# S5's early prompt parts ahead of the sample's projections, its reorder copies on ScalarE, and eight memsets on VectorE

## Chip, core and metric

The kernel runs on one core of one Trainium2 chip. The metric is the device time of one launch in microseconds (us); several runs are taken, and the median counts. Tiles live in the core's on-chip memory, matmuls run on TensorE (PE), and VectorE (DVE), ScalarE (ACT) and GpSimd (POOL) do the elementwise work. Every engine works through a list of its own, in order. SyncE (SP) issues most DMAs, POOL some.

## What is computed

One layer of a hybrid trunk, for a prompt of 4096 frames and for a sample of 32 frames of a running stream. A normalised input h goes through one projection. Half of it feeds a gated delta rule with 4 heads (a 4-tap convolution on q, k and v, then a recurrence in blocks), the other half a diagonal state-space group (S5), each with a gate path; both are joined, mapped by an output projection and added to x.

```
h = rms_norm(x)
q, k, v, beta, gates, z, z5, u = split(h @ W_in)
q, k, v = silu(short_conv(q, k, v))          # 4 taps
S_t = exp(g_t) (I - beta_t k_t k_t^T) S_{t-1} + beta_t k_t v_t^T ;  o_t = S_t^T q_t
x_t = Lbar x_{t-1} + Bbar u_t ;  y_t = Re(C x_t) + D u_t       # S5
y5 = gelu(y) * sigmoid(y @ W_glu + b) * silu(z5)
out = x + concat(o * silu(z), y5) @ W_out
```

## The kernel before, in words

The kernel has three phases. Phase A makes h, stores it, and computes what S5 needs (uts, gy_d and gys_d in DRAM). Phase B, where the change lies, runs the delta rule and the output gate of S5. Phase C is the output projection.

In phase B a small driver (`Drive`) takes pieces of work from generators and emits them: one called `dense`, and four (`chunks`) that share 33 chunks of the recurrence, 128 frames each, with the sample's chunk as number 32. A generator's `yield` says when it may go on, and the driver decides by a model of matmul time which one is next. The order in which it emits is then reordered by the framework's scheduler, so that the final lists of the engines are not the order of the source.

`dense` is a list of block projections and of S5 units in between. `qkv(b)` (L1370) projects 256 frames of block b onto k, q and v, 4 heads each, from two tiles of h that `load_h` (L1358) reads transposed on SP (L1366). `qkv_s` (L1414) does the same for the sample's 32 frames, with gyt and zr as working room. `s5out(k, j)` (L1460) is one S5 unit of 128 frames: gyt is loaded (L1455), zr holds z5 (L1458), gyt is split into two f16 parts gh (L224, L225), four transposes on PE (L53), twelve matmuls with the weights wg (L49), some elementwise work (L1484 to L1495) and a store (L1497). There are 32 such units of the prompt, and one of the sample, whose gyt is first reordered by two copies (L1475, L1476). `useq` is the order of the units; a unit loads the unit that comes two later, because there are two rooms.

z, the gate of the delta rule (L534, `zproj`), is filler for PE with a low priority and a set of transposed h loads of its own (L561). `chunk` (L1512) builds a chunk: bl and dm are loaded on SP (`load_be`, L1505; `load_dm`, L1510), their product br and its mask run on POOL (L1605, L1609), sk and rq_k normalise k and q (L135 to L139 on POOL), the casts kn (L1586) and vb (L1595) run on ACT, then follow products and an inverse by doubling steps on PE and DVE, for which POOL makes a (L1715). Of the inverse tiles p1bd, p1f, ap32 and ap64 there are two each, cleared once by `masks` (L1300, memsets at L1356), before the loops.

Constants: SP = 2 (the sample's chunk comes after two blocks), EARLY = 4, LATE = 4.

Of the kernel before, what the change touches and what calls it, by code (L numbers as in the profile page):

```python
# [26 lines left out]
SP = 2  # L27
# [5 lines left out]
EARLY = 4  # L33
# [47 lines left out]
class Trunk:  # L81
# [1077 lines left out]
    def phase_b(self):  # L1159
        nc, io, cst = self.nc, self.io, self.cst  # L1160
        NB = self.T // 256
        b2 = ExitStack()
        self.ck = self.pool(b2, "b_ck")
        wm = self.pool(b2, "b_m")
        self.pg = [self.pool(b2, f"b_pg{i}", 1, psum=True) for i in range(NI)]
        self.po = self.pool(b2, "b_po", 1, psum=True)
        self.pf = self.pool(b2, "b_pf", 1, psum=True)
        self.S = {}
        for key in ("p", "s"):
            self.S[key] = wm.tile([128, H, 128], F32, name=f"S_{key}")  # L1170
        nc.gpsimd.memset(self.S["p"], 0.0)
        nc.sync.dma_start(self.S["s"], io["state_dn"])
        self.bounds(wm)
        q0 = self.blk[0, "q"]
        nc.gpsimd.tensor_scalar(q0, q0, self.sq["p"], None, op0=ALU.mult)
        self.masks(wm)
        self.ncv = {key: cst.tile([128, 3, 12], F32, name=f"ncv_{key}") for key in ("p", "s")}
        self.nu = 0
        self.front, self.chain, self.busy, self.slots = set(), -1, False, list(range(NI))
        items = [(i, i % 2, i // 2, "p") for i in range(2 * NB)]  # L1180
        items.insert(2 * SP, (self.NC, 0, -1, "s"))
        self.dms, self.sdone = {}, False
        self.order = [i[0] for i in items]
        self.load_be(self.order[0])
        for i in items[:NP]:
            self.load_dm(i[0])
        items = [items[p::NP] for p in range(NP)]
        self.at = [0] * NP
        self.early = list(range(NE))

        def dense():
            units = [(k, j) for k in range(NB // 4) for j in range(8)]
            self.useq = units[:2] + [(-1, 0)] + units[2:]
            late = units[len(units) - LATE:]
            units = units[:len(units) - LATE]
            for b in list(range(1, SP)) + [-1] + list(range(SP, NB)):
                if b == 2:
                    for u in units[:EARLY]:
                        yield from self.s5out(*u)
                    units = units[EARLY:]  # L1200
                if b > 1:
                    yield lambda: {2 * b - 4, 2 * b - 3} <= self.front
                yield from self.qkv(b) if b >= 0 else self.qkv_s()
                for u in units[:2] if b >= 0 else [(-1, 0)]:
                    yield from self.s5out(*u)
                if b >= 0:
                    units = units[2:]
            self.b1.close()
            self.c_weights()
            for u in units + late:  # L1210
                yield from self.s5out(*u)
            self.fn = self.wz.tile([128, 2, 4, 512], F16, name="wg").rearrange("p x c n -> p (x c n)").bitcast(F32)[:, :1024]
            nc.sync.dma_start(self.fn, io["final_norm_w"].partition_broadcast(128))
            xe = [self.hp.tile([128, 8, 272], F16, name=f"h{i % 2}").rearrange("p c n -> p (c n)").bitcast(F32)[:, :1024] for i in range(4)]
            for j, b in enumerate(self.early):
                yield from self.out(b, lambda i: xe[(2 * j + i) % 4],
                                    lambda: self.rm["gh"][:, 0].bitcast(BF16),
                                    lambda: self.pb.tile([128, 512], F32, name="pp"))

        def chunks(par):  # L1220
            for i, (ci, c, b, key) in enumerate(items[par]):
                self.at[par] = ci if key == "p" else 2 * SP - 1
                if (b, "k") not in self.blk:
                    yield lambda: (b, "k") in self.blk
                    yield 3000
                yield from self.chunk(ci, c, b, key, par, items[par][i + 1][0] if i + 1 < len(items[par]) else None)

        self.pe.add(lambda: 1000, dense())
        for p in range(NP):
            self.pe.add(lambda p=p: self.at[p], chunks(p))  # L1230
        self.pe.run()
        for key, nm in (("p", "prompt"), ("s", "sample")):
            pt = self.pg[0].tile([128, H, 128], F32, name="bk")
            nc.tensor.transpose(pt[:36, 0], self.ncv[key].rearrange("p j e -> p (j e)"), self.ident)
            t = self.wk.tile([128, 256], F32, name="acc", bufs=2)[:36, :128]
            nc.scalar.copy(t, pt[:36, 0])  # L1236
            nc.sync.dma_start(io["new_conv_" + nm].rearrange("j (e p) -> (j e) p", p=128), t)
            nc.scalar.activation(self.S[key], self.S[key], AF.Copy, scale=self.usv[key])
            nc.sync.dma_start(io["new_dn_" + nm].rearrange("h k v -> k h v"), self.S[key])
        b2.close()  # L1240
# [59 lines left out]
    def masks(self, wt):  # L1300
        nc, gp = self.nc, self.nc.gpsimd
# [25 lines left out]
        for b in (4, 8, 16):  # L1327

            n = 32 // (2 * b)
            t = wt.tile([128, 32], F16, name=f"lm{b}")  # L1330
# [22 lines left out]
        self.ap32 = [wt.tile([128, H, 4, 32], F16, name=f"ap32{i}") for i in range(NI)]  # L1353
        self.ap64 = [wt.tile([128, H, 128], F16, name=f"ap64{i}") for i in range(NI)]
        for t in self.p1bd + self.p1f + self.ap32 + self.ap64:
            gp.memset(t, 0.0)  # L1356

    def load_h(self, b):  # L1358

# [100 lines left out]
    def s5out(self, k, j):  # L1460


        nc, pe = self.nc, self.pe
        v, gp, act = nc.vector, nc.gpsimd, nc.scalar
        m = 128 if k >= 0 else TS
        at, self.nu = self.nu % 2, self.nu + 1
        gy, zr, gh = self.rm["gyt"][:, at], self.rm["zr"][:, at], self.rm["gh"][:, 0]
        t, m5 = gy, zr
        gy = gy.rearrange("p (o i) -> p o i", o=4)[:, :, :m]
        if self.nu <= 4:  # L1470
            self.s5load(k, j, at, nc.sync)
        if k < 0:

            g = gh.rearrange("p (o i) -> p o i", o=4)[:, :, :m]
            gp.tensor_copy(g.rearrange("p o (i s) -> p o s i", s=8), gy.rearrange("p o (s i) -> p o s i", s=8))  # L1475
            gp.tensor_copy(gy, g)  # L1476
        gh = gh.bitcast(F16).rearrange("p (x o i) -> p x o i", x=2, o=4)[:, :, :, :m]
        self.split(gh[:, 0], gh[:, 1], gy, self.gs)
        pt = self.pb.tile([128, 512], F32, name="pp")[:m]
        for o in range(4):  # L1480
            pe.tr(pt[:, 128 * o:128 * o + 128], gy[:, o], self.ident)
        yield 0
        zr, t = zr[:m], t[:m]
        v.scalar_tensor_tensor(zr, pt, self.ss5[:m], zr, op0=ALU.mult, op1=ALU.mult)  # L1484
        pg = self.pb.tile([128, 512], F32, name="pp")[:m]
        for c in range(4):
            for a, w in ((0, 0), (0, 1), (1, 0)):
                pe.mm(pg, gh[:, a, c], self.w_g[:, w, c], start=c == 0 and a == w == 0, stop=c == 3 and a == 1)
            yield 0
        v.scalar_tensor_tensor(t, pg, self.ug[:m], self.gb[:m], op0=ALU.mult, op1=ALU.add)  # L1490
        act.activation(t, t, AF.Tanh)
        v.scalar_tensor_tensor(t, t, 1.0, zr, op0=ALU.add, op1=ALU.mult)  # L1492
        m5 = m5[:m].bitcast(F16).rearrange("p (x d) -> p x d", x=2)
        act.copy(m5[:, 0], t)
        gp.tensor_tensor(m5[:, 1], t, m5[:, 0], op=ALU.subtract)  # L1495
        dst = self.m5_d[k].rearrange("x (i s) d -> x s i d", s=8)[:, j] if k >= 0 else self.m5s_d
        gp.dma_start(dst.rearrange("x t d -> t x d"), m5)  # L1497
        if 2 < self.nu < len(self.useq) - 1:
            self.s5load(*self.useq[self.nu + 1], at, gp)

    def load_be(self, ci):
# [472 lines left out]
```

## Time and profile before

| | us |
|---|---|
| median of 3 runs (lowest, highest) | 2332.87 (2331.53, 2341.26) |
| the profiled execution | 2318.2 |
| its span in the trace | 2316.5 |
| PE busy in it | 2053.1 (89%) |
| DVE, ACT, POOL busy | 62%, 54%, 42% |
| mean granted TensorE clock | 0.956 |

The profiled execution was 14.7 us faster than the median. The profile gives, for each engine, its instructions in order of time with their lines, the time that the engine sat idle before one and who released it; PEclk is the clock that TensorE was granted, as a share of full speed. SPq is SP's queue of issues: the time there is how long SP was held by issuing, not the transfer.

### The profile page before, as it was taken

How to read it: one execution, taken by the hardware profiler on the slowest of the kernel's cores; microseconds unless marked ns; L12 is line 12 of the kernel's file. 1: busy time of each engine (PE TensorE's matmuls, PEld its weight loads, DVE VectorE, ACT ScalarE, POOL GpSimd, SP SyncE). 2: the span in 40 equal slices, each digit the busy share in tenths (PEclk: the TensorE clock that was granted, in tenths of full speed). 3: DMA queues.
4: the chain of work that ended last, by engine and by line, in shares of the span. 5: the costliest groups of instructions: out<-in, count | busy, mean ns of one | idle time of the engine just before them, and what ended most of it. 6: DMA issues, size and time to landing. Idle time of an engine off the chain costs nothing.

```text
span 2316.5 us, 47857 instructions
## 1 busy us (share of the span) xinstructions
PE 2053.1 (89%) x18304; PEld 1486.0 (64%) x18304; DVE 1443.1 (62%) x3290; ACT 1250.8 (54%) x3695; POOL 983.3 (42%) x1481
## 2 busy tenths in 40 slices
PE   4688889888689999399799999999999888999998
PEld 4344677664457555278688878888888864554443
DVE  4686577559458321368787888788887775543222
ACT  5357556543487221267777777777776774522010
POOL 1344225222201201546676767676776575421000
PEclk9899999998899999799899999999999989999999
DMA  6259958755996554613333322433333154546543
GB/s 199 67 173 242 221 117 199 153 61 114 190 274 200 113 110 108 110 46 80 77 81 71 76 57 69 82 83 83 79 73 55 54 151 124 132 128 178 145 128 94
DMA packets 417263, 277.62 MB, mean 120 GB/s; under 512 B 344796, under 2 KB 364856, under 8 KB 417032
## 3 DMA queue, kind: packets, MB, share of 16 engines
q1 hardware_dynamic: 386840, 186.41, 37.9%
q0 software_dynamic: 25440, 79.49, 12.0%
q10 hardware_dynamic: 4752, 8.65, 1.1%
q8 instruction: 143, 2.34, 0.4%
q14 instruction: 88, 0.72, 0.1%
HBM read 106.46 MB, written 90.29 MB: 85 GB/s over the span
## 4 chain that ended last, share of the span: by engine, by line
PE 39%; issue 10%; DVE 9%; ACT 5%; DMA 4%; POOL 4%; SPq 0%; DVEq 0%; POOLq 0%; ACTq 0%
PE pp L49 23%; PE bk L49 8%; PE pz L534 5%; PE bk L53 2%; DVE acc L1401 2%; ACT jk L1579 1%; DMA gyt<-gy_d 1%; DVE kn L1691 1%; DMA hz<-h_d 1%; PE po L49 1%; DVE gyt L1492 1%; DMA h<-h_d 1%; DMA dm_d<-tdm 0%; ACT acc L1399 0%; DVE ubd L1746 0%
## 5 line engine op out<-in xcount | busy, mean ns | idle before, releaser
L534 PE MATMUL pz<-wz,hz 128*128 128x512 f16 (+1 forms) x1464 | 382.4, 388 | 31.5 <-DMA hz<-h_d 28.8
L1401 DVE SCALAR_TENSOR_TENSOR acc<-pp,cwu,acc 128x256 f32<-128x256 f32 x540 | 254.1, 478 | 60.7 <-ACT acc L1399 53.9
L49 PEld LDWEIGHTS <-mx 128*128 128x128 f16 (+1 forms) x1584 | 152.6, 98 | 185.2 <-issue 9.7
L534 PEld LDWEIGHTS <-hz 128*128 128x128 f16 (+1 forms) x1464 | 142.6, 99 | 191.5 <-DMA hz<-h_d 37.4
L49 PE MATMUL pp<-h,wk 128*128 128x259 f16 (+1 forms) x1632 | 217.5, 272 | 0.1
L542 PE MATMUL pp<-wa,ht 128*128 128x260 f16 x1536 | 192.6, 281 | 21.7 <-ACT wa L224 9.8
L49 PE MATMUL pp<-h,wq 128*128 128x259 f16 (+1 forms) x1632 | 210.4, 271 | 0.1
L49 PE MATMUL pp<-h,wv 128*128 128x259 f16 (+1 forms) x1632 | 206.8, 270 | 1.3 <-DVE acc L1401 0.8
L49 PE MATMUL po<-wo,mx 128*128 128x512 f16 (+1 forms) x912 | 197.2, 379 | 0.8 <-ACT acc L1236 0.8
L542 PEld LDWEIGHTS <-ht 128*128 128x128 f16 x1536 | 151.8, 100 | 49.7 <-issue 20.1
L49 PEld LDWEIGHTS <-wk 128*128 128x128 f16 x1632 | 154.9, 98 | 26.1 <-issue 1.5
L49 PEld LDWEIGHTS <-wq 128*128 128x128 f16 x1632 | 150.7, 98 | 25.4 <-issue 5.7
L49 PEld LDWEIGHTS <-wv 128*128 128x128 f16 x1632 | 147.6, 98 | 22.6 <-DVE wv L225 1.9
L49 PE MATMUL pp<-wo,mx 128*128 128x512 f16 x672 | 153.0, 382 | 5.8 <-DVE zr L1484 5.8
L568 POOL DMA_DIRECT2D z_d<-zt x64 | 36.8, 575 | 233.8 <-DVE zt L567 212.3
L1869 ACT ACTIVATE junk<-xt 128x1024 bf16<-128x1024 f32 (+1 forms) x19 | 20.1, 1056 | 176.4 <-DVE xt L1868 94.6
L49 PE MATMUL pp<-wg,gh 128*128 128x512 f16 (+1 forms) x396 | 103.8, 393 | 6.0 <-ACT gh L224 2.8
L567 DVE SCALAR_TENSOR_TENSOR zt<-zt,pz 128x512 f32<-128x512 f32 (+1 forms) x66 | 44.9, 680 | 95.8 <-ACT zt L566 95.5
L1868 DVE SCALAR_TENSOR_TENSOR xt<-po,uo,xt 128x512 f32<-128x512 f32 (+1 forms) x38 | 28.4, 749 | 116.0 <-PE po L49 111.8
L1399 ACT ACTIVATE acc<-pp,cwu 128x256 f32<-128x256 f32 x180 | 84.5, 479 | 29.3 <-PE pp L49 28.5
L960 POOL DMA_DIRECT2D gy_d<-vv x128 | 67.6, 535 | 75.9 <-ACT vv L955 40.5
L1579 ACT ACTIVATE jk<-bk 128x128 bf16<-128x128 f32 x264 | 74.9, 284 | 38.9 <-PE bk L53 33.1
(618 smaller groups left out, 5041.2 us busy)
## 6 DMA issues: line engine op xcount, KB each, us to landing
xn<-in_x SPq DMA_DIRECT2D x32, 512.0 KB, 4.7
h_d<-hl POOLq DMA_DIRECT2D x32, 512.0 KB, 5.4
z_d<-zt POOLq DMA_DIRECT2D x64, 256.0 KB, 3.8
xt<-in_x SPq DMA_DIRECT2D x18, 512.0 KB, 4.6
out_y<-xt SPq DMA_DIRECT2D x18, 512.0 KB, 2.7
dm_d<-tdm ACTq DMA_DIRECT2D x33, 256.0 KB, 4.7
dm<-dm_d SPq DMA_DIRECT2D x33, 256.0 KB, 2.7
gy_d<-vv POOLq DMA_DIRECT2D x128, 64.0 KB, 4.0
```

Of the source, the lines that this page charges most:

```text
L49: return self.nc.tensor.matmul(out, lhs, rhs, start=start, stop=stop)
L53: return self.nc.tensor.transpose(out, src, ident)
L534: self.nc.tensor.matmul(ps, a[x][:, c], w[:, y, c], start=c == 0 and x == y == 0, stop=c == K - 1 and x == 1)
L542: self.nc.tensor.matmul(pu[hf][:, :260], ht[x][:, c, :m], self.w_a[:, y, c, 260 * hf:260 * hf + 260], start=c == 0 and x == y == 0, stop=c ...
L567: nc.vector.scalar_tensor_tensor(zt, zt, 1.0, pz, op0=ALU.add, op1=ALU.mult)
L568: nc.gpsimd.dma_start(rows(dst[0][blk]) if blk >= 0 else dst[1], zt)
L960: gp.dma_start(gy[s], gn[16 * s:16 * s + 16, :, :128])
L1399: nc.scalar.activation(acc, ps[:, 0:n], AF.Copy, scale=cw[:, e, 0:1])
L1401: v.scalar_tensor_tensor(acc, ps[:, j:j + n], cw[:, e, j:j + 1], acc, op0=ALU.mult, op1=ALU.add)
L1492: v.scalar_tensor_tensor(t, t, 1.0, zr, op0=ALU.add, op1=ALU.mult)
L1579: act.activation(junk, src[:, h], AF.Square, accum_out=out[:, h:h + 1])
L1868: v.scalar_tensor_tensor(xt[:m, sl], ps, self.uo[:m], xt[:m, sl], op0=ALU.mult, op1=ALU.add)
```

## The change

Three edits. (1) `dense` puts the four early units of S5's prompt part, which followed the sample's projection, directly behind the first two units of block 1, ahead of `qkv_s`. The list `useq` has them in the same order, and the set `ufirst` names the units that load their own inputs on SP when they start, among them the sample's unit and the one after it; all other units are loaded by the unit two before. (2) The two copies that reorder the sample's gyt run on ScalarE. (3) The eight memsets run on VectorE. After L1197 the lines of the changed kernel are one lower.

```diff
         def dense():
             units = [(k, j) for k in range(NB // 4) for j in range(8)]
-            self.useq = units[:2] + [(-1, 0)] + units[2:]
+            n = (SP - 1) * 2 + EARLY
+            self.useq = units[:n] + [(-1, 0)] + units[n:]
+
+            self.ufirst = {0, 1, n, n + 1}
             late = units[len(units) - LATE:]
             units = units[:len(units) - LATE]
             for b in list(range(1, SP)) + [-1] + list(range(SP, NB)):
-                if b == 2:
-                    for u in units[:EARLY]:
-                        yield from self.s5out(*u)
-                    units = units[EARLY:]
                 if b > 1:
                     yield lambda: {2 * b - 4, 2 * b - 3} <= self.front
                 yield from self.qkv(b) if b >= 0 else self.qkv_s()
-                for u in units[:2] if b >= 0 else [(-1, 0)]:
+                n = 0 if b < 0 else 2 + EARLY if b == 1 else 2
+                for u in units[:n] if b >= 0 else [(-1, 0)]:
                     yield from self.s5out(*u)
-                if b >= 0:
-                    units = units[2:]
+                units = units[n:]
...
-            gp.memset(t, 0.0)
+            nc.vector.memset(t, 0.0)
...
-        if self.nu <= 4:
+        if self.nu - 1 in self.ufirst:
             self.s5load(k, j, at, nc.sync)
...
-            gp.tensor_copy(g.rearrange("p o (i s) -> p o s i", s=8), gy.rearrange("p o (s i) -> p o s i", s=8))
-            gp.tensor_copy(gy, g)
+            act.copy(g.rearrange("p o (i s) -> p o s i", s=8), gy.rearrange("p o (s i) -> p o s i", s=8))
+            act.copy(gy, g)
...
-        if 2 < self.nu < len(self.useq) - 1:
+        if self.nu + 1 < len(self.useq) and self.nu + 1 not in self.ufirst:
             self.s5load(*self.useq[self.nu + 1], at, gp)
```

SP's list behind the loads of z: bl and dm are a chunk's inputs, h0 and h1 the two transposed tiles of a block, gys_d and z5s_d the sample's S5 inputs, gy_d0 the prompt's. Before:

```order
L1510 DMA dm_9309<-dm_d2_127 128x512
L1510 DMA dm_9311<-dm_d3_128 128x512
L1366 DMA_TRANSPOSE h0_10631<-h_d0_78 128x8x256
L1366 DMA_TRANSPOSE h1_10633<-h_d0_78 128x8x256
L1505 DMA bl_9525<-be_d_123 128x4x128
L1455 DMA gyt_9136<-gys_d_90 128x4x32
L1458 DMA zr_9137<-z5s_d_100 32x512
L1455 DMA gyt_9136<-gy_d0_86 128x4x128
L1510 DMA dm_10883<-dm_d32_157 128x512
L1366 DMA_TRANSPOSE h0_11796<-h_d0_78 128x8x256
L1505 DMA bl_9962<-be_d_123 128x4x128
L1366 DMA_TRANSPOSE h1_11798<-h_d0_78 128x8x256
```

And with the change:

```order
L1509 DMA dm_10881<-dm_d32_157 128x512
L1365 DMA_TRANSPOSE h0_10608<-h_d0_78 128x8x256
L1504 DMA bl_9525<-be_d_123 128x4x128
L1365 DMA_TRANSPOSE h1_10610<-h_d0_78 128x8x256
L1365 DMA_TRANSPOSE h0_11796<-h_d0_78 128x8x256
L1454 DMA gyt_9136<-gys_d_90 128x4x32
L1365 DMA_TRANSPOSE h1_11798<-h_d0_78 128x8x256
L1504 DMA bl_9964<-be_d_123 128x4x128
L1457 DMA zr_9137<-z5s_d_100 32x512
L1454 DMA gyt_9136<-gy_d0_86 128x4x128
L1457 DMA zr_9137<-z5_d0_96 128x512
```

The sample's load (gyt from gys_d) stood behind the two tiles of block 2; it now stands behind these and the first tile of block 3, and the next bl behind both tiles of block 3.

POOL's list around the sample's copies (L1475, L1476) and the normalisation rq_k of chunk 0. Before:

```order
L1605 TENSOR_TENSOR br_9338<-bl,dm 128x512
L1475 COPY gh<-gyt 128x4x8x4
L136 TENSOR_TENSOR rqt_k<-rq_k 128x4
L1609 AFFINE_SELECT br_9338<-br_9338 128x512
L1476 COPY gyt<-gh 128x4x32
L137 TENSOR_TENSOR rqt_k<-rqt_k,sk_9314 128x4
L138 TENSOR_SCALAR rqt_k<-rqt_k 128x4
L1605 TENSOR_TENSOR br_9544<-bl,dm 128x512
L139 TENSOR_TENSOR rq_k<-rq_k,rqt_k 128x4
L1609 AFFINE_SELECT br_9544<-br_9544 128x512
L1603 TENSOR_TENSOR tp<-kn_9333,ed 128x512
L1605 TENSOR_TENSOR br_9545<-bl,dm 128x512
```

And with the change:

```order
L136 TENSOR_TENSOR rqt_k<-rq_k 128x4
L1608 AFFINE_SELECT br_9338<-br_9338 128x512
L1446 TENSOR_SCALAR kqvs<-kqvs,sg_s 128x128
L137 TENSOR_TENSOR rqt_k<-rqt_k,sk_9314 128x4
L138 TENSOR_SCALAR rqt_k<-rqt_k 128x4
L139 TENSOR_TENSOR rq_k<-rq_k,rqt_k 128x4
L1604 TENSOR_TENSOR br_9544<-bl,dm 128x512
L1602 TENSOR_TENSOR tp<-kn_9333,ed 128x512
L1608 AFFINE_SELECT br_9544<-br_9544 128x512
L1604 TENSOR_TENSOR br_9545<-bl,dm 128x512
L1608 AFFINE_SELECT br_9545<-br_9545 128x512
L1543 TENSOR_TENSOR kn_9333<-tp,kn_9333 128x512
```

The copies are gone, and the last step of rq_k (L139) has moved ahead of the product br_9544.

ScalarE's list at the end of the sample's convolution (zr from gyt at L1443). Before:

```order
L1443 ACTIVATE zr<-gyt 128x384
L224 ACTIVATE gh<-gyt,gs 128x4x32
L1586 ACTIVATE kn_9333<-bk,rq_k 128x128 x4
L224 ACTIVATE gh<-gyt,gs 128x512
L1595 ACTIVATE vb_9463<-bk,hbC 128x128 x4
```

And with the change:

```order
L1442 ACTIVATE zr<-gyt 128x384
L1474 COPY gh<-gyt 128x4x8x4
L1475 COPY gyt<-gh 128x4x32
L224 ACTIVATE gh<-gyt,gs 128x4x32
L1585 ACTIVATE kn_9333<-bk,rq_k 128x128 x4
```

The two copies stand ahead of the split of gh, and so ahead of the casts of kn_9333 (chunk 0).

## Rows read from the trace of the kernel before

**Rows 1.** The page: span, busy sums and PE's busy tenths in 40 slices.

```profile
span 2316.5 us, 47857 instructions
...
PE 2053.1 (89%) x18304; PEld 1486.0 (64%) x18304; DVE 1443.1 (62%) x3290; ACT 1250.8 (54%) x3695; POOL 983.3 (42%) x1481
...
PE   4688889888689999399799999999999888999998
```

**Rows 2.** Stretches: length; busy (count) of PE, PEld, DVE, ACT, POOL; granted clock; DMA; GB/s.

```profile
900.00:940.00 40.00, 29.80 (x333) 16.56 (x331) 10.13 (x12) 7.86 (x21) 12.76 (x19) 0.90 0.52 105
940.00:980.00 40.00, 14.54 (x84) 7.94 (x85) 10.24 (x17) 8.91 (x22) 17.46 (x24) 0.71 0.54 91
980.00:1020.00 40.00, 34.55 (x305) 25.40 (x304) 24.76 (x54) 21.68 (x71) 21.58 (x29) 0.91 0.26 80
1020.00:1100.00 80.00, 80.00 (x925) 69.94 (x923) 62.34 (x155) 59.27 (x179) 45.23 (x69) 1.00 0.23 57
1100.00:1140.00 40.00, 32.32 (x364) 27.59 (x363) 26.86 (x63) 27.06 (x83) 26.47 (x35) 0.92 0.39 87
1140.00:1180.00 40.00, 33.58 (x418) 30.27 (x417) 30.51 (x78) 31.28 (x105) 27.95 (x38) 0.91 0.18 49
```

**Rows 3.** Timeline of PE: start, us, engine, line, op, tiles, shapes, count [idle <-releaser].

```profile
925.68 2.57 PE L49 MATMUL pp<-h,wv 128*128 128x32 f16 x96
...
937.39 1.33 PE L49 MATMUL bk<-sp,gr 128*128 128x128 f16 x11 [7.13 <-POOL sp L1544]
952.16 1.03 PE L53 MATMUL pp<-ident,gyt 128*32 128x128 f32 x4 [13.43 <-POOL gyt L1476]
...
986.39 0.64 PE L53 MATMUL pp<-ident,gyt 128*128 128x128 f32 x4
...
989.38 2.33 PE L49 MATMUL pp<-wg,gh 128*128 128x512 f16 x10 [0.42 <-DVE gh L225]
...
997.66 3.96 PE L49 MATMUL pp<-h,wk 128*128 128x259 f16 x21
```

**Rows 4.** Timeline of SP's queue, same columns, from the end of z.

```profile
924.40 0.37 SPq L1505 DMA_DIRECT2D bl<-be_d  x1
924.83 5.29 SPq L1510 DMA_DIRECT2D dm<-dm_d  x4
930.21 9.20 SPq L1366 DMA_TRANSPOSE h<-h_d  x2
...
940.13 0.46 SPq L1455 DMA_DIRECT2D gyt<-gys_d  x1
...
942.28 9.85 SPq L1366 DMA_TRANSPOSE h<-h_d  x1
...
952.80 7.75 SPq L1366 DMA_TRANSPOSE h<-h_d  x1
```

**Rows 5.** Timeline of SP's queue later in phase B.

```profile
1097.17 2.06 SPq L1366 DMA_TRANSPOSE h<-h_d  x1
...
1100.38 9.67 SPq L1366 DMA_TRANSPOSE h<-h_d  x1
```

**Rows 6.** Timeline of POOL around the sample's copies.

```profile
950.80 0.40 POOL L1475 COPY gh<-gyt 128x128 f32<-128x128 f32 x1
...
977.79 1.15 POOL L1715 TENSOR_TENSOR a<-br,bd 128x512 f16<-128x512 f32 x1
```

**Rows 7.** Timeline of ACT, the casts of kn.

```profile
962.26 1.14 ACT L1586 ACTIVATE kn<-bk,rq_k 128x128 f32<-128x128 f32 x4 [9.72 <-POOL rq_k L139]
```

**Rows 8.** Line L1356 by itself: count, ns min/median/max.

```profile
L1356 POOL MEMSET ap<- x4: 519/536/555, 732.7 to 734.2; 128x512 f16 x4
```

**Rows 9.** DMA issues of 860 to 1010: count, KB, median us to landing.

```profile
gyt<-gy_d POOLq DMA_DIRECT2D x4, 256.0 KB, 3.5
...
gyt<-gys_d SPq DMA_DIRECT2D x1, 64.0 KB, 10.4
```

**Rows 10.** Busy time of 1123 to 1155, columns as in the second group.

```profile
1123.00:1155.00 32.00, 21.19 (x267) 19.21 (x265) 23.41 (x56) 23.90 (x86) 22.20 (x32) 0.79 0.14 43
```

## Prediction

> **What bounds the kernel now.** I read the page first. TensorE (PE) is busy for 2053.1 of 2316.5 us, and of its 40 slices the one that stands out inside phase B is the seventeenth, the single "3" after a run of 9s, at about 926 to 984 us [rows 1]. So the question is what fills or empties that hole, and whether the rest of phase B lets PE keep what it wins there. The busy times by stretch size it: PE is idle for 10.2 us of 900 to 940, 25.5 us of 940 to 980 and 5.4 us of 980 to 1020, 41.1 us together; then it is full (80.00 of 80) to 1100; and 7.7 and 6.4 us, 14.1 together, are idle in 1100 to 1180 [rows 2].
>
> PE's timeline shows what the hole is made of. The sample's projections end at 925.68 + 2.57 = 928.25; PE then waits 7.13 us for the sum on POOL and 13.43 us for the sample's reordered gyt; units of S5 come in pieces from then on, and the first matmul of the next block's projections, qkv(2), stands at 997.66 [rows 3]. PE runs its list in order, so everything behind the sample's transposes at 952.16 waits for that one tile.
>
> Why the tile is late stands in SP's queue. The last z transfers let SP go at 924.40; four dm loads take it 5.29 us and two transposed loads of h 9.20 us, so that the load of the sample's tile is issued only at 940.13 [rows 4], and it lands after another 10.4 us [rows 9]. That is 950.6, and POOL's copy starts at 950.80, in 0.40 us [rows 6]. A transposed load of h costs SP between 2.06 and 9.85 us: the second of two close ones is the long one (9.67 after 2.06) [rows 4, 5].
>
> **The change part by part.** The durations come from the profiled execution (2318.2 us, span 2316.5), which lies 14.7 us below the median of the three runs, 2332.87; the sum is a difference, and I put it on the median.
>
> *Memsets.* Eight go from POOL to VectorE. On POOL one takes 0.54 us, 4.3 us in all, near 732 us, and nothing is shown to wait for them [rows 8]. On VectorE I bound one between nothing and the same 0.54 us. PE works on projections there that VectorE feeds, so the cost is between -1 and +4 us; I take 0, since a few halves of a microsecond spread over that stretch should hide under PE's queue. If PE were out of work there it would cost up to 4.
>
> *Reorder copies.* Two copies of 0.40 us or less leave POOL [rows 6] for ScalarE. The bound is 0 to 1 us, since ScalarE was idle for 9.72 us just ahead of the casts of kn [rows 7]; I take 0. But they carry a wait: in the new order they stand on ScalarE right ahead of the casts of kn (L1585), on which chunk 0 hangs, so ScalarE holds chunk 0 until the sample's tile has landed. Its price is in the chain term below.
>
> *The four units.* A unit costs PE four transposes (0.64) and twelve matmuls (ten take 2.33, so 2.8), about 3.4 us back to back, a little under 3 where they overlap other work [rows 3]. Four, some 12 us, go ahead of the end of the sample's projections: 928.25 + 12 = about 940. Their loads add four gyt issues on POOL and four zr issues on SP between the transposed loads of z, where both queues run ahead; I cost these at 0, hidden by PE's z work, with an upper bound of the 3.5 us that one such load takes to land [rows 9].
>
> *SP's queue.* The new order puts the sample's load behind three transposed loads of h and not two, and the first of them must wait for the end of the sample's projections, because it reuses their h tile: 940. The first takes about 2, the load of bl 0.5, then h1 at the long price, 9.67 [rows 5], and the next h0 between 7.75 and 9.85 [rows 4]: 940 + 2 + 0.5 + 9.7 + 8 = 960. With 3.5 to 10.4 us to landing [rows 9] the tile is there at 964 to 971. With the transposes at 3 to 4 us each, which the first of a pair shows to be possible, it is 954 to 961.
>
> *PE's hole.* It now reaches from 940 to 964 to 971, 24 to 31 us, instead of 41.1 idle us in pieces. Behind the sample's tile there are no units to wait for any more, and qkv(2) fills PE; I leave 4 us for the start. Gain of PE: 41.1 - (28 to 35) = 6 to 13, middle 10. The clock adds a little: PE was granted 0.71 of full speed on the mean over 940 to 980, between its two levels, and 0.91 over the next 40 us [rows 2], which cost the 14.54 and 34.55 busy us there about 4 and 3 us; half of that, 3, should be saved when the pieces become one hole.
>
> *The chunks' chain.* The casts of kn waited 9.72 us for POOL's rq_k [rows 7], which stood behind a product that waits for bl; now it stands ahead of that product, so this wait goes, but what is late next is ScalarE, held for the sample's tile until 964 to 971, where kn started at 962.26. Chunk 0 and its neighbours also need the third and fourth bl, behind the same transposes on SP. The load of the third bl comes after the fourth transposed load, at about 970, and lands at 979; the fourth follows it. The product a of chunk 0 on POOL stood at 977.79 [rows 6]; I expect it at about 990, 12 us late. Some of that is made up while PE has only qkv(2) beside it; 8 us remain. From 1123 to 1155 PE holds only chunk work (21.19 busy of 32) [rows 10]: there the chain, not PE, sets the pace, and a lead of the projections is spent waiting. I let the late chain take back three quarters of its 8 us, 6.
>
> Sum: -10 - 3 + 6 = -7 us, 2332.87 - 7 = 2326.
>
> **The rivals.**
>
> *A, the hole shrinks and nothing takes it back.* SP's transposes at 3 to 4 us each: tile at 954 to 961, hole 14 to 21 us and 4 for the start, gain 41.1 - (18 to 25) = 16 to 23, the clock's 3 on top, and a chain late by 4 us or less: about -19, 2314. For it speaks that PE is full for 80 us behind the hole, so a lead can be used [rows 2]; against it the three transposed loads of 7.75 us and more. The Trainium skill, "DMA: Bandwidth & Descriptors", section "Issuing engines are not separate DMA queues", says that spreading DMAs over issuing engines saves only the sequencer's time to start them, usually small beside the transfer. By that rule the extra transpose ahead of the sample's load would cost next to nothing, and A would hold. The trace disagrees: one issue held SP for 9.85 us [rows 4], about as long as the sample's load took to land. Because the long transposes are three of the four near the hole, A gets a smaller chance than my own case.
>
> *B, slower.* The mechanism is one: the sample's tile behind three transposes, with ScalarE held for it. If the transposes take 9.85 us each and the load lands after 10.4, the tile is there at 940 + 2 + 0.5 + 9.9 + 9.9 + 10.4 = 973, the fourth bl near 990 and product a near 996, 18 us late. If the chain also sets the pace from there to 1180, of which the idle 14.1 us in 1100 to 1180 are the sign, 13 or so of the 18 stay: 2346. It decides if product a comes later than about 991 and PE is no fuller than before in 1000 to 1120. Against it: PE full in 1020 to 1100, where the chain waits for PE.
>
> *C, no change.* The projections win, reach the stretch of pure chunk work sooner and wait there instead: the 10 to 13 us of idle time move from 940 to beyond 1100. Time 2333.
>
> **How the numbers follow.** My case has a chance of 0.45, with a range of its own of 2319 to 2334; A 0.30; B 0.13; C 0.12. What a measurement can tell from no change is about 0.5%, 11.7 us: faster is under 2321.2, slower above 2344.5. Faster takes A but for its slow edge (0.29) and the fast edge of my case (0.08): 0.37. Slower takes most of B, 0.11. The same is the rest, 0.52. The range reaches from A's fast half, 2309, to B's middle, 2345.
>
> **What would show it.** Right: the four units' matmuls among z's, the end of the sample's projections at about 940; one hole of PE to about 967; SP's issue of the sample's load at about 960, with three transposed loads between the bl loads and it; ScalarE's first copy idle until that lands; the first qkv(2) matmul near 970 instead of 997.66; product a near 990; more idle time in 1100 to 1180. If SP issues that load before 953, A has come. If product a is later than 995 and PE is idle for over 20 us in 1100 to 1180, B. If the memsets matter, PE will show idle time waiting for VectorE at 725 to 760. My sum is wrong if PE's whole idle time over 900 to 1180 falls by more than 25 us, or rises.

## The result, and the profile of the changed kernel

The change makes the kernel slower: 2349.51 us (median of 12 runs, 2339.88 to 2355.03) against 2335.94 us (12 runs of before, 2331.40 to 2343.26), ratio 1.0051 with a 95% interval of 1.0033 to 1.0069. The forecast was 2326 us; the measured time lies outside the range on the slow side.

The profiled execution of the changed kernel took 2350.95 us, span 2349.2, 32.7 us more than that of before. Not all of it is the change: the first glu matmul of the first S5 unit, ahead of which only the memsets differ, starts at 881.88 where before had 868.95, so 12.9 us are older than everything around the hole. (The profiled execution of before, 2318.2, was well under its own median.) Over the fourteen profiled executions of this study that matmul starts anywhere from 868.95 to 881.88. Times of the two traces are therefore compared from it on.

The page of the changed kernel, its sums and PE's busy tenths, answering to [rows 1]:

```profile
span 2349.2 us, 47879 instructions
...
PE 2066.5 (88%) x18304; PEld 1494.9 (64%) x18304; DVE 1453.1 (62%) x3298; ACT 1250.0 (53%) x3697; POOL 974.8 (41%) x1471
...
PE   5688889878689999679799999999999988999998
```

The busy times by stretch, with the windows of [rows 2] moved by 13 us (length; busy of PE, PEld, DVE, ACT, POOL; granted clock; DMA share; GB/s):

```profile
913.00:953.00 40.00, 35.65 (x337) 18.59 (x335) 14.19 (x19) 13.31 (x28) 14.95 (x18) 1.00 0.59 136
953.00:993.00 40.00, 20.43 (x219) 14.90 (x220) 11.14 (x20) 8.26 (x22) 14.39 (x25) 0.66 0.47 103
993.00:1033.00 40.00, 29.00 (x317) 24.54 (x315) 23.07 (x57) 20.14 (x73) 19.80 (x25) 0.87 0.09 23
1033.00:1113.00 80.00, 75.20 (x857) 64.22 (x857) 63.03 (x151) 58.38 (x182) 47.77 (x71) 1.00 0.29 69
1113.00:1153.00 40.00, 31.44 (x350) 27.30 (x349) 23.41 (x55) 25.37 (x78) 28.26 (x37) 0.81 0.24 68
1153.00:1193.00 40.00, 33.87 (x420) 29.70 (x418) 30.89 (x81) 30.88 (x106) 25.05 (x35) 0.94 0.17 49
```

In the first three stretches PE is idle for 4.4, 19.6 and 11.0 us, 34.9 in place of 41.1; in the next, which was full, for 4.8; and in the last two for 14.7 in place of 14.1. Over the whole 280 us PE's idle time is about 1 us less. The granted clock has not gained over the first three stretches either (1.00, 0.66, 0.87 for 0.90, 0.71, 0.91). The rest of the rows around the hole are PE's timeline, SP's and POOL's product a, answering to [rows 3, 4, 6]:

```profile
957.25 1.44 PE L49 MATMUL bk<-sp,gr 128*128 128x128 f16 x12
975.60 1.03 PE L53 MATMUL pp<-ident,gyt 128*32 128x128 f32 x4 [16.91 <-ACT gyt L1475]
...
977.53 3.59 PE L49 MATMUL pp<-h,wk 128*128 128x259 f16 x17
```

```profile
957.42 1.76 SPq L1365 DMA_TRANSPOSE h<-h_d  x1
959.29 0.52 SPq L1504 DMA_DIRECT2D bl<-be_d  x1
959.85 11.95 SPq L1365 DMA_TRANSPOSE h<-h_d  x2
971.97 0.46 SPq L1454 DMA_DIRECT2D gyt<-gys_d  x1
```

```profile
1000.11 1.19 POOL L1714 TENSOR_TENSOR a<-br,bd 128x512 f16<-128x512 f32 x1
```

One hole of 16.91 us, ended by the sample's tile, as forecast; SP held by the transposed loads until 971.8, as forecast; qkv(2) at 977.53, which with 12.9 taken off is 964.6 where before had 997.66 [rows 3].

So where is the loss? I took the start of the same matmul in both traces, for all that both have. The median lag of the changed kernel against before:

| place in before's trace, us | lag, us |
|---|---|
| 868.95, first unit | +12.9 |
| 1180 to 1300 | +10.9 to +10.7 |
| 1400 to 1420 | +10.5 |
| 1500 to 1520 | +16.9 |
| 1600 to 1620 | +20.5 |
| 1700 to 1720 | +30.0 |
| 1800 to 1820 | +32.8 |
| end | +32.7 |

Around the hole the change wins 2 us; behind 1400 us, where no edit is, it loses 22.

That is a place I had not read. The scheduler works through the whole program with a simulated time of its own, and gives the lists another order there too: from the middle of phase B to its end (1302.8 to 2107.5 us in before's trace), PE's two lists differ in several hundred of each twentieth of their rows (of 915 or so), although what the source emits there is the same, instruction for instruction.

### The profile page after: what moved, and what is told of

Same layout as the page of the kernel before. It is cut to its first block, busy times and chain, and to the rows that moved or that the text cites. A ratio compares the mean times of both kernels' runs of the same rounds, so it can differ in the third digit from the quotient of the medians.

```text
span 2349.2 us, 47879 instructions
## 1 busy us (share of the span) xinstructions
PE 2066.5 (88%) x18304; PEld 1494.9 (64%) x18304; DVE 1453.1 (62%) x3298; ACT 1250.0 (53%) x3697; POOL 974.8 (41%) x1471
## 4 chain that ended last, share of the span: by engine, by line
PE 31%; issue 8%; DVE 6%; ACT 6%; POOL 3%; DMA 3%; SPq 1%; DVEq 0%; POOLq 0%; ACTq 0%
PE pp L49 20%; PE bk L49 7%; PE bk L53 2%; DVE acc L1400 2%; PE po L49 1%; DMA gyt<-gy_d 1%; ACT jk L1578 1%; DVE kn L1690 1%; SPq L1851 1%; DMA wo<-wo_d 1%; ACT acc L1398 1%; ACT br L1665 0%; DMA zr<-z5s_d 0%; SPq L1853 0%; DMA bl<-be_d 0%
## 5 line engine op out<-in xcount | busy, mean ns | idle before, releaser
L49 PE MATMUL pp<-h,wq 128*128 128x259 f16 (+1 forms) x1632 | 205.7, 273 | 3.6 <-DVE acc L1400 3.5
L49 PE MATMUL pp<-h,wk 128*128 128x259 f16 (+1 forms) x1632 | 204.1, 272 | 1.0 <-DVE zr L1483 0.9
L542 PEld LDWEIGHTS <-ht 128*128 128x128 f16 x1536 | 153.4, 101 | 51.2 <-issue 20.5
L49 PEld LDWEIGHTS <-wk 128*128 128x128 f16 x1632 | 149.6, 98 | 32.0 <-issue 7.1
```

The costliest lines, as they stand in the source:

```text
L49: return self.nc.tensor.matmul(out, lhs, rhs, start=start, stop=stop)
L542: self.nc.tensor.matmul(pu[hf][:, :260], ht[x][:, c, :m], self.w_a[:, y, c, 260 * hf:260 * hf + 260], start=c == 0 and x == y == 0, stop=c ...
```

## The experiments

Two theories were put against each other. **L**: the later order of the lists, another in each variant, makes the loss; the part around the hole is a gain. **Q**: the sample's tile, late on SP's queue and with ScalarE held for it, makes the chunks late, and the lag is carried on. Q is the slow rival of the prediction. Each ratio below is against runs of before on the same chip (medians of before 2325.43 to 2326.70).

### One edit at a time

**e1_memsets**

```diff
-            gp.memset(t, 0.0)
+            nc.vector.memset(t, 0.0)
```

> Edit 3 alone (the eight memsets on VectorE); every list of PE is that of before except 48 rows near 740 us. All theories that put the loss elsewhere expect the ratio to before at 1.000 within 0.002. The theory that the memsets cost (VectorE feeds PE there) expects 1.002 to 1.005 and PE idle for VectorE at 725 to 760.

Measured: 2326.38 us, ratio 0.9997 (0.9980 to 1.0014). The memsets cost nothing that can be measured; by the interval, 4 us at most. In the trace one takes 0.27 us on VectorE.

**e2_copies**

```diff
-            gp.tensor_copy(g.rearrange("p o (i s) -> p o s i", s=8), gy.rearrange("p o (s i) -> p o s i", s=8))
-            gp.tensor_copy(gy, g)
+            act.copy(g.rearrange("p o (i s) -> p o s i", s=8), gy.rearrange("p o (s i) -> p o s i", s=8))
+            act.copy(gy, g)
```

> Edit 2 alone (the two reorder copies on ScalarE). PE's list is that of before up to two fifths of its rows, past the hole, and then differs in hundreds of places, as the scheduler gave it. Theory L (the late order of phase B, another in every variant, sets the loss): the stretch up to 1180 us is the same within 2 us, and whatever the ratio is (0.995 to 1.010) comes from behind 1200 us. Theory Q (the sample's tile late on SP and ScalarE held for it): 1.000 within 0.002, since the tile is not later here.

Measured: 2337.29 us, ratio 1.0045 (1.0030 to 1.0060). Two copies of 0.4 us, which leave the sample's tile where it was, cost as much as the whole change. In the trace the lag against before is +4.0 us at 900 us, +5.7 at 1080 to 1160, +9.8 at 1180 to 1200, where PE's list has begun to differ, and +18.0 at the end. It also speaks against Q: counted from the first unit, the sample's transposes come at 81.1 us (83.2 before), and the casts of chunk 0 at 82.8 (93.3 before), so the tile and the chunk were sooner, and the kernel was slower.

**e3_no_memset**

```diff
-            nc.vector.memset(t, 0.0)
+            gp.memset(t, 0.0)
```

> The change without edit 3 (memsets stay on POOL); PE's list is that of the changed kernel except the 48 rows near 740 us. Theory L and theory Q: ratio 1.005 like the changed kernel, within 0.002. The memset theory: 1.000 to 1.003.

Measured: 2336.20 us, ratio 1.0046 (1.0031 to 1.0060), that of the changed kernel.

**e8_order_alone** is edit 1 alone, the changed kernel with both other edits undone.

```diff
-            nc.vector.memset(t, 0.0)
+            gp.memset(t, 0.0)
...
-            act.copy(gy, g)
+            gp.tensor_copy(gy, g)
```

> Edit 1 alone (the four units ahead of the sample's projections; copies and memsets stay on POOL). The scheduler gives it a later order that is neither that of before nor that of the changed kernel. Theory L: up to 1180 us a gain of 2 to 6 us, then whatever its later order is worth, 0 to 25 us lost; the ratio lies between 0.998 and 1.009. Theory Q: with the copies on POOL, ScalarE is not held, chunk 0 is sooner than in the changed kernel, and the ratio is 1.000 to 1.003.

Measured: 2336.46 us, ratio 1.0040 (1.0024 to 1.0056). Its lag fell from +3.4 us at the first unit to -1.3 (median of 1100 to 1200 us), a gain of 4.7 as L has it; from 1200 to 1300 it was back at +1.7, and at the end at +22.8.

### The sample's tile sooner

**e4_act_queue**

```diff
-            self.s5load(k, j, at, nc.sync)
+            self.s5load(k, j, at, act if k < 0 else nc.sync)
```

> The changed kernel with one thing altered: the sample's gyt is loaded from ScalarE's DMA queue and not from SP's, so that it no longer stands behind three transposed loads of h. PE's list is exactly that of the changed kernel. Theory Q: the tile lands 5 to 10 us sooner, the hole shrinks by as much, and the ratio falls from 1.005 to 1.001 or less. Theory L: the hole shrinks too, the late order is the same, and most of the loss stays: 1.002 to 1.005.

Measured: 2338.45 us, ratio 1.0044 (1.0028 to 1.0060): not faster than the changed kernel. ScalarE's rows, the load on its queue and the copy that waited for it, and PE's sample transposes:

```profile
956.80 0.38 ACTq L1454 DMA_DIRECT2D gyt<-gys_d  x1
...
967.47 0.41 ACT L1474 COPY gh<-gyt 128x128 f32<-128x128 f32 x1 [9.60 <-DMA gyt<-gys_d]
```

```profile
968.26 1.03 PE L53 MATMUL pp<-ident,gyt 128*32 128x128 f32 x4 [15.24 <-ACT gyt L1475]
```

```profile
994.81 1.20 POOL L1714 TENSOR_TENSOR a<-br,bd 128x512 f16<-128x512 f32 x1
```

From the first unit (879.3 here, 881.9 in the changed kernel) to the sample's transposes it is 89.0 us against 93.7: the tile is 4.7 us sooner, product a comes 115.5 us behind the first unit instead of 118.2, and the loss stays. Q falls.

### The later order put by hand

These take the place of the scheduler's choice for all that is emitted from block 5 on: each instruction of an engine is chained behind the one that stands before it in a given list. The table LATER holds that list.

```diff
+def replay(tc, nc):
+    by = {i.name: i for i in nc.cur_bb.bb.instructions}
+    for text in LATER.values():
+        order = np.cumsum(np.frombuffer(zlib.decompress(base64.b85decode(text)), dtype="<i4"))
+        for p, n in zip(order[:-1], order[1:]):
+            tc.add_manual_dep(by[f"I-{n}"], f"I-{p}",
+                              mybir.DependencyInfo(mybir.DependencyClass.NoSync, mybir.DependencyReason.DATA),
+                              reason="later order")
...
             trunk(ctx, tc, aps, T)
+            replay(tc, nc)
```

**e5_later_as_before**: this in the changed kernel, with the later lists of before.

> The changed kernel, with the later part of every engine's list (what is emitted from block 5 on) put into the order that before has there; the earlier part, with the hole and the sample's tile, stays the changed one. Theory L: the loss goes and the early gain stays, ratio 0.997 to 0.9995, and in the trace nothing is lost behind 1300 us. Theory Q (the loss is made at the sample's tile and carried on): the ratio stays at 1.004 to 1.005.

Measured: 2321.23 us, ratio 0.9968 (0.9949 to 0.9986).

**e6_later_as_after**: this in before, with the later lists of the changed kernel.

> Before, with the later part of every engine's list put into the order that the changed kernel has there; nothing else is changed. Theory L: slower by the loss without the early gain, ratio 1.006 to 1.009, lost between 1300 and 1700 us. Theory Q: 1.000 within 0.002.

Measured: 2342.96 us, ratio 1.0067 (1.0047 to 1.0087).

**e7_act_queue_later_as_before**: e5 with the edit of e4.

> The changed kernel with the sample's gyt loaded from ScalarE's DMA queue, and the later part of every list in the order of before. Theory L: the shorter hole now shows in the time, ratio 0.996 to 0.999, 1 to 3 us under the run with the later order of before alone. Theory Q: also under 1.000, since the tile is sooner; this run tells what the sooner tile is worth and not which theory holds.

Measured: 2317.42 us, ratio 0.9955 (0.9940 to 0.9971). It is the fastest version of this study, 9.3 us under before.

Early part and later part can be exchanged, and each brings its own price along. The table gives, for each profiled execution, the us between the starts of the same matmuls: the first glu matmul of the first unit, then the 577th, 961st and 1249th projection of k (the one of the sample counted in), the last one, and the end of the last output matmul.

| kernel | early list, later list | to 577th | to 961st | to 1249th | to last | to end |
|---|---|---|---|---|---|---|
| before | before, before | 325.0 | 255.2 | 188.2 | 196.4 | 472.6 |
| e1 | before, before | 328.4 | 253.1 | 188.2 | 196.8 | 474.5 |
| e5 | changed, before | 323.1 | 252.7 | 190.3 | 197.0 | 472.3 |
| e7 | changed, before | 321.2 | 255.2 | 189.0 | 196.4 | 474.2 |
| changed kernel | changed, changed | 323.0 | 256.5 | 198.4 | 211.4 | 467.9 |
| e3 | changed, changed | 321.7 | 256.2 | 198.6 | 207.6 | 466.4 |
| e4 | changed, changed | 319.8 | 255.7 | 198.8 | 209.1 | 468.1 |
| e6 | before, changed | 323.1 | 254.5 | 197.0 | 207.9 | 468.3 |

The changed early list is worth some 4 us in the first column (mean of its five rows 321.8, of the other three 325.5), about as much as single rows of one list differ by (319.8 to 323.1, and 323.1 to 328.4). Of the changed later list against that of before, four rows each, the means differ by 1.7, 9.3, 12.4 and -5.7 us in the other columns: some 18 us, whichever early list stands ahead of it. A kernel with its own order chained in was not run; that the chaining itself costs next to nothing is read from the table, where the four later columns add up to 1112.4 us in before and 1112.3 in e5, to 1128.8 in e3 and 1127.7 in e6.

### Which half

**e9_first_half_as_before** and **e10_second_half_as_before** replay only PE's list, composed of the two: in e9 that of before up to the 1249th projection of k and that of the changed kernel behind, in e10 the reverse. PE's list alone brings the others along: a scheduler that is held to it chooses nearly the same orders elsewhere.

```diff
-LATER = {'PE': ..., 'DVE': ..., 'Activation': ..., 'Pool': ..., 'SP': ...}
+LATER = {'PE': ...}
```

> The changed kernel with PE's later list in the order of before up to the middle of the stretch in which time is lost (the 1249th projection matmul of k, near 1640 us), and in its own order behind that. Theory L with a loss spread over the whole stretch: ratio 1.000 to 1.003, half way between 0.997 and 1.005, and the loss begins behind 1640 us. A single bad place in the first half: 0.997; in the second half: 1.005.

Measured: 2320.26 us, ratio 0.9976 (0.9960 to 0.9992).

> The reverse: PE's later list in the order of the changed kernel up to that place, and in the order of before behind it. Spread loss: 1.000 to 1.003, lost before 1640 us and then steady. A single bad place in the first half: 1.005; in the second half: 0.997.

Measured: 2328.27 us, ratio 1.0026 (1.0007 to 1.0046). Against e5's 0.9968 the first half of the changed list costs 0.006, the second half 0.001, each uncertain by some 0.0025. Most of the loss is made ahead of the 1249th projection; how much is not settled, since in the table above, where the whole later list is the changed one, the two columns ahead of that place hold 11.0 of the 17.7 us and the two behind it 6.7. In the traces (medians of 100 us) e9 keeps a lag of -1.8 to -2.1 us against before from 1200 to 1700 us and ends at +0.7; e10 goes from -5.6 at 1200 to +8.3 at 1600 and keeps that. Neither expected case holds quite: it is no even spread, and no single place, since e10 loses its 14 us bit by bit from 1400 to 1650.

What such a stretch loses is seen in e4 and e5, which have the same early list. From the 961st to the 1249th projection, first e5 (before's order), then e4 (the changed one):

```profile
1449.80:1640.10 190.30, 180.13 (x2118) 156.13 (x2117) 153.95 (x362) 141.71 (x455) 133.47 (x186) 0.99 0.35 76
```

```profile
1454.80:1653.60 198.80, 184.42 (x2113) 159.09 (x2112) 160.77 (x361) 140.84 (x454) 131.29 (x186) 0.97 0.32 73
```

Nearly the same matmuls (2118 and 2113), 8.5 us more: 4.2 us more idle (190.30 - 180.13 against 198.80 - 184.42), and 4.3 us more busy, at a mean granted clock of 0.97 instead of 0.99. One place shows much of the busy part. It is the same piece of the chunks in both, PE's timeline; e5 first:

```profile
1610.51 2.85 PE L49 MATMUL pp<-h,wv 128*128 128x259 f16 x24
1613.18 0.83 PE L49 MATMUL bk<-gr,knT 128*128 128x128 f16 x12
...
1619.57 0.83 PE L49 MATMUL bk<-knT,dm 128*128 128x128 f16 x12 [0.34 <-ACT br L1665]
...
1621.40 0.22 PE L49 MATMUL bk<-Tf,al 128*128 128x128 f16 x1
...
1622.34 1.84 PE L49 MATMUL pp<-h,wv 128*128 128x259 f16 x15
```

and e4:

```profile
1623.83 0.94 PE L49 MATMUL pp<-h,wv 128*128 128x259 f16 x7
1624.87 0.25 PE L49 MATMUL bk<-p,uf 128*128 128x32 f16 x4
...
1632.60 0.27 PE L49 MATMUL bk<-knT,dm 128*128 128x128 f16 x1 [0.88 <-ACT br L1665]
...
1632.87 0.31 PE L49 MATMUL bk<-Tf,al 128*128 128x128 f16 x1
...
1635.33 1.38 PE L49 MATMUL bk<-knT,dm 128*128 128x128 f16 x11
...
1637.40 1.50 PE L49 MATMUL pp<-h,wv 128*128 128x259 f16 x12
```

The busy times of the two pieces, e5 and then e4:

```profile
1613.18:1622.34 9.16, 6.67 (x118) 6.03 (x116) 7.19 (x21) 7.21 (x27) 4.43 (x6) 1.00 0.17 51
```

```profile
1624.87:1637.40 12.53, 9.50 (x120) 8.44 (x120) 10.19 (x23) 10.72 (x37) 7.03 (x9) 0.73 0.20 63
```

Between two projections PE has only steps of the chunks here, some of which wait for VectorE, ScalarE or POOL. In before's order the piece lasts 9.2 us, in the changed one 12.5 us, and of the 3.4 us between them PE is busy for 2.8 and idle for 0.5. So it is mostly the clock: at its lower level one 128x128 matmul takes 0.31 us and not 0.22, and eleven take 1.38 us where twelve took 0.83. This is not one execution's accident. In the four kernels of the table with the changed later list the piece takes 12.3 to 12.5 us at a granted clock of 0.73 (0.86 in e6); in the four with the list of before it takes 9.2 us at 1.00, but for e7 with 10.6 at 0.85. Why the clock falls in one order and not in the other is not shown; PE's idle time within the piece is nearly the same (3.0 and 2.5 us).

### Other orders

**e11_reroll_cast**

```diff
-        act.copy(m5[:, 0], t)
+        act.copy(m5[:, 0], t) if k >= 0 else v.tensor_copy(m5[:, 0], t)
```

> The changed kernel with one small copy of the sample's unit (a 32x512 cast) on VectorE and not on ScalarE, which by itself moves half a microsecond, but gives a third later order. If the later order of before is a well chosen one and others are worse as a rule, this one loses 5 to 20 us behind 1200 us: ratio 1.000 to 1.007. If good and bad orders are about as frequent, it is as likely at 0.997 as at 1.005.

Measured: 2328.53 us, ratio 1.0016 (0.9999 to 1.0033).

**e12_reroll_pool_queue**

```diff
-            self.s5load(k, j, at, nc.sync)
+            self.s5load(k, j, at, gp if k < 0 else nc.sync)
```

> The changed kernel with the sample's gyt loaded from POOL's DMA queue, which gives yet another later order. The sample's tile is sooner, as with ScalarE's queue, worth some 2 us; behind 1200 us the same two readings as for the run before: 5 to 20 us lost (ratio 0.999 to 1.006) if other orders are worse as a rule, 0.996 otherwise.

Measured: 2325.14 us, ratio 1.0003 (0.9988 to 1.0019). The first half of what was expected did not come: the load stood late on POOL's list too, and the sample's transposes came 94.9 us behind the first unit, against 93.7 in the changed kernel. Both runs are therefore set against e5 (0.9968), which has nearly the same early edits with the later order of before: e11 lies above it by 0.0048, e12 by 0.0035. Of five later orders that the scheduler made in this study (the changed kernel's, and those of e2, e8, e11 and e12) none was as good as that of before: the four later columns of the table add up to 1119 us for e2, 1133 for e8, 1125 for e11 and 1117 for e12, and to 1128 to 1134 for the changed list, against 1112 to 1115 for that of before.

## Why the prediction was wrong

**The four units and the hole**: right, and all of it a little sooner than forecast. The times are those of e3, the run whose first unit starts within half a microsecond of before's:

```profile
945.20 12.61 SPq L1365 DMA_TRANSPOSE h<-h_d  x2
958.00 0.44 SPq L1454 DMA_DIRECT2D gyt<-gys_d  x1
```

```profile
961.65 1.03 PE L53 MATMUL pp<-ident,gyt 128*32 128x128 f32 x4 [18.09 <-ACT gyt L1475]
...
963.58 3.64 PE L49 MATMUL pp<-h,wk 128*128 128x259 f16 x17
```

```profile
986.42 1.18 POOL L1714 TENSOR_TENSOR a<-br,bd 128x512 f16<-128x512 f32 x1
```

SP issued the sample's load at 958.0; forecast 960. The sample's transposes came at 961.65 (forecast: tile there at 964 to 971; the load took at most 2.8 us to land, where 3.5 to 10.4 had been put), the first qkv(2) matmul at 963.6 (forecast near 970), product a at 986.42 (forecast about 990).

**The sum**: its sign is confirmed by e5, in which only the part that I had read is changed: 0.9968 of 2326.70 is -7.4 us (interval -12 to -3), forecast -7. That the size fits so closely is in part luck, for its terms do not. PE's idle time over the hole fell by 6.2 us, the low end of the 6 to 13 forecast, of which I had taken 10. The clock's 3 us are not there: worked as in the prediction, the lower clock cost 10.3 us of PE's busy time over the first three stretches before and 10.7 in the changed kernel. Idle time behind the hole rose by 5.4 us, near the 6 that I gave to the chain, but 4.8 of it in the 80 us that had been full and not in 1100 to 1180. Together PE's idle time fell by 1 us, and the first column of the table gives a gain of some 4 us.

**Memsets**: 0 forecast, 0.9997 measured. **Reorder copies**: 0 forecast. Alone they cost 0.0045, though their own time is nothing: the cost shows where the list differs. I did not run them with the later order of before, so what they cost by themselves remains untested.

**The step that failed** is the sum itself, "-10 - 3 + 6": it holds three terms from 900 to 1180 us and takes the rest of the program as unchanged. The lists of the engines show that it isn't. A term for the later order was missing, and measured it is 15.6 us (e6, 0.0067 of 2326.70), or some 19 as the difference between the changed kernel and e5 (0.0083), and 18 in the table of the traces. It turned a gain of 7 us into a loss of 12.

**Rival B**, slower by the late tile, had the sign but not the cause: with the tile 4.7 us sooner (e4) the time was that of the changed kernel, and with the later order of before (e5) it was faster than before with the tile just as late. B's condition, product a later than 991, did not come about (986.42 in e3). **Rival C**, that idle time moves to beyond 1100, holds in part: the pieces in 1113 to 1193 are as they were, while 4.8 us appear in 1033 to 1113. **Rival A** needed short transposed loads; two took 11.95 us together.

The Trainium skill, "DMA: Bandwidth & Descriptors", section "Issuing engines are not separate DMA queues", was weighed with A: another issuing engine saves only the time to start a DMA, which the page calls usually small. That time was not small here: on SP the two transposed loads ahead of the sample's load held the queue for 11.95 us. In e4 the load was issued on ScalarE's queue while SP was still busy with them, 12.6 us sooner (77.5 us behind the first unit against 90.1), but its copy began only 10.7 us behind the issue, where on SP it was 2.8 us (issued at 971.97, copy at 974.75); so 4.7 us were left. In time these gave 0.9955 (e7) against 0.9968 (e5), and the intervals overlap.

What stays open is which feature of an order makes it good. I did not find a count over the list that ranks the orders as the runs do.

## What to carry to other kernels

Where a scheduler decides the order, compare the lists to their end, not only to where they first meet again: here a change at 40% of the program re-ordered most of the second half of PE's list, and that cost about twice what the change won. An edit can draw a new order for the untouched part (the two copies alone did, the memsets alone did not), and the order at hand can be better than the next ones, as it was here against five, so an edit is judged by holding that order fixed. Fixing it kept 7 us of a change that by itself lost 12, and 10 with the sample's load on ScalarE's queue.

## What the runs showed of the hardware

TensorE's clock can fall to its lower level (1.2 for 2.4 GHz) inside a stretch that is busy on the whole. In e4 PE was busy for 23.78 of the 24 us from 1600 to 1624, at a granted clock of 1.00, and for 4.18 of the next 6 us, at 0.99; from 1630 to 1637.4 the clock was 0.54, though PE was busy for 6.09 of these 7.4 us. The same 128x128 matmul is recorded with 0.31 us there and 0.22 us in e5.

A pair of transposed loads of h held SP's queue for 11.95 us in the changed kernel and 12.61 us in e3. The 64 KB load of the sample's tile, issued behind them, was there within 2.8 us in both; issued on ScalarE's queue beside them it took 10.7 us (e4).
